# Attention values by halves of 64 queries: a 64-slot mask in place of a 128-slot one

## The chip, the cores and the metric

The kernel runs on one core of one Trainium2 chip. The metric is the time of one execution in microseconds of the device; the number to compare is the median of several runs. Engines are named as the profile names them: PE (matmul), PEld (its weight loads), DVE (vector), ACT (scalar), POOL (GpSimd) and SP (which issues most of the transfers). SBUF is the memory on the core, PSUM the accumulators that PE writes.

## The reference, cut to what matters

One decoder block on a sequence of 1024 tokens of width 1024: an adaptive norm, one wide projection, sliding-window attention with sinks in one branch and a gated recurrence in the other, both projected, merged and projected out. The change is in the attention: 16 query heads of 64, four key/value heads, each query sees itself and the 127 tokens before it.

```python
WINDOW = BLOCK = 128
qb = q.reshape(B, nb, BLOCK, N_KV_HEADS, G, hd)            # nb = 8 blocks of 128 queries, G = 4
kb = concat([kp[:, :-1], kp[:, 1:]], axis=2)               # the block's own keys and those before
s = einsum('bnqkgd,bnskd->bnkgqs', qb, kb) / sqrt(hd)      # 128 queries x 256 keys
diff = qi + BLOCK - kj
band = (diff >= 0) & (diff < WINDOW)                       # and kpos >= 0
s = where(mask, s, -1e30)
m = maximum(max(s, axis=-1), sink)
p = exp(s - m)
denom = sum(p, axis=-1) + exp(sink - m)
o = einsum('bnkgqs,bnskd->bnqkgd', p / denom, vb)
```

So each query has exactly 128 keys in its window (fewer in the first block), out of the 256 of its block and the one before.

## The kernel before, in words

Everything is in 32-bit floats; a product of two such operands is made of three PE products, since each operand is split into a high part and the rest (`split_a` on ACT casts, `split_d` on DVE subtracts). The order of instructions on PE, ACT, DVE, POOL and SP is the order of the source; tiles wait for each other by semaphores.

The kernel goes through the wide projection first (lines 688 to 776, 56 to 600 us), in "pairs" of weight chunks. Along with it, `v_prep(g)` takes the values of one key/value head group from the projection, and for each of eight blocks of 128 keys stores two tables in device memory: `vs` holds the values, and `dv` the difference between a block's values and those of the block before it. Both are `[128 keys, 8 blocks, 128]`: 64 columns of high parts and 64 of the rest. A row of a partition is 4 KB.

The attention has 32 units `u`: four groups `g`, in each eight blocks `n` of 128 queries. A unit does four heads. The loop over `u` (line 1626) is software-pipelined by hand; one turn holds, in the order in which the engines get them:

- `scores(u)`: eight PE products into one PSUM tile `s_ps` of 4 heads x 256 keys (for `n` = 0 only the last 128).
- `maxima_a(u)`: ACT copies the keys of the block itself out of PSUM into `p` (4 x 128 slots and one for the sink). `maxima_d(u)`: DVE puts over it, where the mask `mgt` says that the slot's own key is still to come, the key 128 earlier, which is in the same slot of the block before. So 256 keys become 128 slots, each with one key in the window. For `n` = 0 a POOL select writes -1e30 instead. Then DVE takes the maximum.
- `weights_a(u-1)`: ACT makes four exponentials with sums. `weights_d(u-1)`: DVE divides.
- a piece of another projection on PE (12 products of 512 columns), whose weights SP loads and ACT and DVE split.
- `values(u-3)`, `join_a`, `join_d`: the products with the values into PSUM tile `pv`, and the sum of its halves, ACT and DVE.
- `transposed(u-2)`, `split_a`, `split_d`: PE transposes the weights into PSUM tile `pt`, ACT and DVE split them into `phc` and `plc`.
- `masks(u-2)`: POOL selects the slots which hold a key of the block itself out of `phc` and `plc`, into `phm` and `plm`.

A slot's weight belongs to a key of the block before (value `vs` of that block) or of this one. So the values are one product of all weights with the former block's `vs`, and one of the masked weights with the difference `dv`, each for the high and the low part of the weights: four PE products of 512 columns (4 heads x 128 queries) with 128 slots in the contraction. For `n` = 0 all weights go with `dv` of block 0, two products. `load_v(m)` brings `vs` and `dv` for two units, issued from POOL's queue after `values`; `load_kq(m)` does so for keys and queries on SP's queue. The PSUM tiles `s_ps`, `pt` and `pv` exist once each.

The mask `mgt` is made by POOL early (lines 590 to 594), ahead of four loads of the rotary tables on POOL's queue.

Of the kernel before, what the change touches and what calls it, by code (L numbers as in the profile page):

```python
# [52 lines left out]
def tile_hybrid_block(ctx, tc, x, x_t, pk, rows, posr, posi, c_row, w_ss, w_gate, w_main, w_v,  # L53
# [72 lines left out]
    cs4_d = tc.dram_tile([24, 4, S], F32, name="cs4_d")  # L126
    k_d = tc.dram_tile([512, S], F32, name="k_d")
    v_d = tc.dram_tile([P, 8, NG, 64], F32, name="v_d")
    vs_d = [tc.dram_tile([P, 8, P], F32, name=f"vs_d{g}") for g in range(NG)]
    dv_d = [tc.dram_tile([P, 8, P], F32, name=f"dv_d{g}") for g in range(NG)]  # L130
    gate_d = tc.dram_tile([1, D], F32, name="gate_d")
    q_d = [tc.dram_tile([512, S], F32, name=f"q_d{g}") for g in range(NG)]
    ga_d = [tc.dram_tile([2, P, S], F32, name=f"ga_d{g}") for g in range(NG)]
# [440 lines left out]
    def operand_low(t):  # L574
# [3 lines left out]
        for lst, o in ((NT1, one), (NT3, two)) if t < 4 else ((NT4, one), (T2, two)):  # L578
# [7 lines left out]
    ctab = rpp.tile([P, S], F32, name="ctab")  # L586
    stab = rpp.tile([64, S], F32, name="stab")
    G.memset(ctab[64:128, :], 1.0)
    W["mgt"] = const.tile([P, P], U32, name="mgt")
    mf = rpp.tile([P, HALF], F32, tag="rh", name="mf", bufs=2)[:, :P]  # L590
    G.memset(mf, 1.0)
    G.affine_select(out=mf, in_=mf, pattern=[[1, P]], compare_op=ALU.is_gt, fill=0.0, base=0,
                    channel_multiplier=-1)
    G.tensor_copy(W["mgt"][:], mf)
# [595 lines left out]
    def v_prep(g):  # L1190
        t = {}
        vpp = W["vpp"]

        def f0():
            t["v"] = vpp.tile([P, 8, 64], F32, tag="v32", name="v32")
            dma(t["v"][:], v_d[:, :, g, :])

        def f1():
            t["d"] = vpp.tile([P, 8, 64], F32, tag="d32", name="d32")
            V.tensor_tensor(out=t["d"][:, 1:8, :], in0=t["v"][:, 1:8, :],  # L1200
                            in1=t["v"][:, 0:7, :], op=ALU.subtract)
            V.tensor_copy(t["d"][:, 0, :], t["v"][:, 0, :])

        def f2():
            for n_ in ("vs", "dv"):
                t[n_] = vpp.tile([P, 8, P], F32R, tag=n_, name=n_)
            A.copy(t["vs"][:, :, 0:64], t["v"][:])
            A.copy(t["dv"][:, :, 0:64], t["d"][:])

        def f3():  # L1210
            for n_, d_, dst in (("v", "vs", vs_d), ("d", "dv", dv_d)):
                V.tensor_tensor(out=t[d_][:, :, 64:128], in0=t[n_][:],
                                in1=f32(t[d_][:, :, 0:64]), op=ALU.subtract)
# [32 lines left out]
        dma(qs[:], q_d[g].rearrange("(a j) t -> a j t", j=4)[:, :, t0:t0 + 256])  # L1246
        U["kq", m] = ks, qs

    def load_v(m):
        g, n0 = m // 4, (m % 4) * 2  # L1250
        vs = at.tile([P, 2, P], F32R, tag="vs", name="vs", bufs=2)
        dv = at.tile([P, 2, P], F32R, tag="dv", name="dv", bufs=2)
        dma(dv[:], dv_d[g][:, n0:n0 + 2, :], G)
        lo = 0 if n0 else 1
        dma(vs[:, lo:, :], vs_d[g][:, n0 - 1 + lo:n0 + 1, :], G)
        U["v", m] = vs, dv

    def sink(u):
        px = at.tile([P, 4, P + 1], F32, tag="p", name="p", bufs=3)
# [19 lines left out]

    def maxima_a(u):  # L1280
        s_ps, px, sm = U["s", u]
        A.copy(px[:, :, 0:P], s_ps[:, :, P:])

    def maxima_d(u):
        s_ps, px, sm = U["s", u]
        p = px[:, :, 0:P]
        if u % 8:
            V.copy_predicated(p, W["mgt"][:].unsqueeze(1).to_broadcast([P, 4, P]),
                              s_ps[:, :, 0:P])
        else:  # L1290
            G.affine_select(out=p, in_=p, pattern=[[0, 4], [-1, P]], compare_op=ALU.is_ge,
                            fill=-1e30, base=0, channel_multiplier=1)
        V.tensor_reduce(out=sm[:, 0, :], in_=px[:], axis=AX.X, op=ALU.max, negate=True)

    def weights_a(u):
# [28 lines left out]
        U["m", u] = phc, plc  # L1324

    def masks(u):
        phc, plc = U["m", u]
        ms = []
        if u % 8:
            for s_, tag in ((phc, "phm"), (plc, "plm")):  # L1330
                d_ = at.tile([P, 4, P], F32R, tag=tag, name=tag)
                G.affine_select(out=d_[:], in_=f32(s_[:]), pattern=[[0, 4], [1, P]],
                                compare_op=ALU.is_ge, fill=0.0, base=0,
                                channel_multiplier=-1)
                ms.append(d_)
        U["m", u] = [phc, plc], ms

    def values(u):
        n = u % 8
        vs, dv = U["v", u // 2]  # L1340
        full, masked = U.pop(("m", u))
        prods = [((vs if n else dv)[:, n % 2, :], m) for m in full]
        prods += [(dv[:, n % 2, :], m) for m in masked]
        pv = psx.tile([P, 4 * P], F32, tag="v", name="pv")
        for i, (b, m) in enumerate(prods):
            W["pe"] = T.matmul(pv[:], b, m[:].rearrange("p j q -> p (j q)"),  # L1346
                               start=(i == 0), stop=(i == len(prods) - 1))
        U["pv", u] = [pv[:].rearrange("p (a e q) -> p a e q", a=2, e=2)]
        if n % 2 == 0 and u // 2 + 1 < 16:
            load_v(u // 2 + 1)  # L1350
# [275 lines left out]
    for u in range(32 + 3):  # L1626
# [458 lines left out]
```

## Time and profile before

| | us |
|---|---|
| median of 3 runs | 909.19 (907.67 to 910.17) |
| the profiled execution: time | 909.08 |
| its span on the core | 907.4 |
| PE busy | 889.1 |
| DVE busy | 725.8 |
| ACT busy | 554.9 |
| POOL busy | 124.7 |

The granted PE clock is 0.999 of full speed. The profile's page gives the busy time of each engine, the busy tenths of 40 slices of the span, the transfer queues, the chain of work that ended last (followed back from the end to what released each step), the costliest groups of instructions by line, and the transfers by size and time to landing. A group's row reads: line, engine, operation, output<-inputs, shapes, count | busy us, mean ns of one | idle time of the engine just before, and who ended it. Further views of the same execution give the chain in order of time, the instructions of one stretch, the waits, and the busy time by stretch.

### The profile page before, as it was taken

Reading aid. Unit: us, or ns where it says so; the run is one execution under the profiler, and the core shown is the slowest. Engines: PE = TensorE matmul, PEld = TensorE weight load, DVE = VectorE, ACT = ScalarE, POOL = GpSimd, SP = SyncE. Lnnn points to the kernel's source line nnn. Section 1 sums busy time; section 2 is a strip of 40 time slices with the busy share of each in tenths; the row PEclk is TensorE's granted clock in tenths of the full one; section 3 lists DMA queues with packets and bytes.
Section 4 is the critical chain, followed back from the end, with each engine's and each line's share of the span. In section 5 each row is a group of like instructions: output and inputs, shape, how many; then the busy total and the mean of one; then the engine's idle time right before and its main releaser. Section 6 shows DMA issues by size and latency. Waiting matters only on the chain.

```text
span 907.4 us, 12605 instructions
## 1 busy us (share of the span) xinstructions
PE 889.1 (98%) x4171; PEld 739.2 (81%) x4171; DVE 725.8 (80%) x1158; ACT 554.9 (61%) x1097; POOL 124.7 (14%) x204
## 2 busy tenths in 40 slices
PE   5999999999999999999999999999999999999997
PEld 3879888878888788878887888888888888888885
DVE  7988799698669974987698476899999846779875
ACT  6754675455556745774767685888888731114555
POOL 0120000000110000000100001354443421310002
PEclk9999999999999999999999999999999999999999
DMA  9951786862534360345345257996666258879314
GB/s 348 404 203 68 253 272 223 294 219 97 180 121 151 130 218 24 129 155 180 107 155 183 85 194 254 328 370 211 214 201 212 85 182 322 315 272 346 110 47 186
DMA packets 88882, 182.57 MB, mean 201 GB/s; under 512 B 14049, under 2 KB 30433, under 8 KB 88818
## 3 DMA queue, kind: packets, MB, share of 16 engines
q1 hardware_dynamic: 82192, 162.09, 51.8%
q0 software_dynamic: 6336, 19.37, 5.9%
q8 instruction: 33, 0.54, 0.3%
q10 hardware_dynamic: 290, 0.32, 0.1%
q14 instruction: 31, 0.25, 0.1%
HBM read 125.01 MB, written 57.12 MB: 201 GB/s over the span
## 4 chain that ended last, share of the span: by engine, by line
PE 86%; DVE 6%; DMA 3%; ACT 2%; issue 2%; SPq 0%; POOL 0%; DVEq 0%; ACTq 0%
PE bk L696 41%; PE rp L174 14%; PE bo L1857 7%; PE pmain L174 6%; PE pgate L992 5%; PE s_ps L1274 3%; PE pv L1346 3%; DMA r<-w_main 2%; PE pt L1312 2%; PE bk L174 1%; DVE wl L110 1%; PE bk L1520 1%; PE bk L1519 1%; PE bk L1518 1%; DMA wada<-w_ss 1%
## 5 line engine op out<-in xcount | busy, mean ns | idle before, releaser
L696 PE MATMUL bk<-nh,wl 128*128 128x512 f32 x368 | 143.9, 391 | 0.5 <-DVE wl L110 0.4
L696 PE MATMUL bk<-nh,wh 128*128 128x512 f32 x368 | 143.4, 390 | 0.0
L696 PE MATMUL bk<-nl,wh 128*128 128x512 f32 x368 | 143.2, 389 | 0.0
L696 PEld LDWEIGHTS bk<-nh,wl 128*128 128x128 f32 x368 | 69.1, 188 | 16.7 <-DVE wl L110 2.1
L696 PEld LDWEIGHTS bk<-nh,wh 128*128 128x128 f32 x368 | 69.1, 188 | 14.4 <-ACT rhi L626 0.2
L696 PEld LDWEIGHTS bk<-nl,wh 128*128 128x128 f32 x368 | 69.1, 188 | 14.4
L110 DVE TENSOR_TENSOR wl<-r,wh 128x512 fp32r<-128x512 f32 x112 | 80.1, 729 | 0.0
L60 POOL DMA_DIRECT2D wq_d<-wq x32 | 21.9, 685 | 407.2 <-DVE wq L1172 392.6
L104 ACT CAST wh<-r 128x512 fp32r<-128x512 f32 x112 | 68.0, 617 | 8.8 <-DMA r<-w_ap 5.1
L696 PE MATMUL bk<-hh,wh 128*128 128x512 f32 x184 | 71.6, 389 | 0.0
L696 PE MATMUL bk<-hh,wl 128*128 128x512 f32 x184 | 71.6, 389 | 0.0
L696 PE MATMUL bk<-hl,wh 128*128 128x512 f32 x184 | 71.6, 389 | 0.0
L110 DVE TENSOR_TENSOR wl<-ws,wh 128x512 fp32r<-128x512 f32 x80 | 54.8, 686 | 4.3 <-ACT wh L104 4.2
L104 ACT CAST wh<-ws 128x512 fp32r<-128x512 f32 x80 | 48.2, 614 | 3.3 <-PE bk L1520 2.7
L1298 ACT ACTIVATE p<-p,small 128x129 f32<-128x129 f32 x128 | 50.1, 401 | 0.0
L799 ACT ACTIVATE c<-bk 128x512 f32<-128x512 f32 x31 | 18.5, 595 | 44.0 <-PE bk L696 43.9
L696 PEld LDWEIGHTS bk<-hl,wh 128*128 128x128 f32 x184 | 34.5, 188 | 7.2
L696 PEld LDWEIGHTS bk<-hh,wl 128*128 128x128 f32 x184 | 34.5, 188 | 7.1
L696 PEld LDWEIGHTS bk<-hh,wh 128*128 128x128 f32 x184 | 34.5, 188 | 7.1
L1857 PE MATMUL bo<-wh,sum 128*128 128x512 f32 x128 | 39.6, 389 | 0.0
L1274 PE MATMUL s_ps<-ks,qs 128*128 128x256 f32 (+1 forms) x256 | 37.6, 289 | 0.0
L696 PE MATMUL bk<-hha,wl 128*128 128x512 f32 x92 | 36.1, 393 | 0.6 <-DVE wl L110 0.6
(409 smaller groups left out, 2290.1 us busy)
## 6 DMA issues: line engine op xcount, KB each, us to landing
r<-w_main SPq DMA_DIRECT2D x100, 256.0 KB, 4.3
wada<-w_ss SPq DMA_DIRECT2D x16, 512.5 KB, 9.3
qs<-q_d SPq DMA_DIRECT2D x16, 512.0 KB, 5.8
wq_d<-wq POOLq DMA_DIRECT2D x24, 256.0 KB, 2.8
wr<-wq_d SPq DMA_DIRECT2D x24, 256.0 KB, 5.0
ks<-k_d SPq DMA_DIRECT2D x24, 192.0 KB, 4.2
wq<-w_out POOLq DMA_DIRECT2D x16, 256.0 KB, 5.2
q_d<-rhi SPq DMA_DIRECT2D x16, 256.0 KB, 3.6
```

What stands on the lines that cost most here:

```text
L60: return eng.dma_start(dst, src)
L104: A.copy(dst[0][:], src)
L110: V.tensor_tensor(out=dst[1][:], in0=src, in1=f32(dst[0][:]), op=ALU.subtract)
L174: mm = T.matmul(ps[hf], ww, xx[kc][hf], start=(kc == 0 and ww is w_h and xx is xh), stop=(kc == KC - 1 and xx is xl))
L696: W["pe"] = T.matmul(ps, ww[:, c], b[kc][xx_], start=(first and kc == 0 and i == 0), stop=(kc == 3 and i == 2), skip_group_check=not first)
L799: A.activation(t["t"], s(), AF.Tanh, scale=0.5)
L992: W["pe"] = T.matmul(ps[:, SL[hf]], ww[:, c0:c0 + P], xx_[:, SL[hf]], start=(ic == 0 and i == 0), stop=(ic == 1 and i == 2))
L1274: W["pe"] = T.matmul(o, qs[:, j, qc], ks[:, b, k0 + (0 if n else P):k0 + 256], start=(b == 0), stop=(b == 1))
L1298: A.activation(px[:, j, :], px[:, j, :], AF.Exp, bias=sm[:, 0, j:j + 1], accum_out=sm[:, 1, j:j + 1])
L1312: W["pe"] = T.transpose(pt[:, j, :], px[:, j, 0:P], ident[:])
L1346: W["pe"] = T.matmul(pv[:], b, m[:].rearrange("p j q -> p (j q)"), start=(i == 0), stop=(i == len(prods) - 1))
L1857: T.matmul(bank[p][i] if dst is None else dst, a[:, ts_], b[:][:, sl], start=(new and kc == 0 and j == 0), stop=(kc == 3 and j == 2), skip ...
```

## The change

The 128 queries of a unit are taken as two halves of 64. A half has 128 slots again, but 64 of them hold keys that every query of the half sees; only the other 64 need a mask. For the first half of the queries the slots are keys 0 to 127 of the 256, for the second half keys 64 to 191; in both, slots 0 to 63 are overlaid with the 64 keys that follow, where those are in the window.

- Tables: `vs_d` and `dv_d` become `[18, 64, 128]` in device memory: 16 blocks of 64 keys, and two blocks of zeros ahead, which POOL's queue writes at the start from a `zero` tile. `v_prep` still makes 128-key blocks and stores them in pieces of one 512-byte row each.
- Loads: `load_v(u)` brings, for one unit, `vb` (per half of queries the 128 values in slot order; in the second half the two 64-key blocks lie swapped over the partitions) and `vd`, the differences, once on each half of the partitions. Four transfers per unit on SP's queue, three buffers, issued between `join_a` and `join_d`.
- `maxima_a`: two ACT copies, one for each half of the partitions (three for `n` = 0). `maxima_d`: two predicated DVE copies of 64 partitions x 4 heads x 64 keys, with the mask `mle`; for `n` = 0 a POOL memset and two POOL selects.
- `masks`: two POOL selects of 64 partitions, the high part into partitions 0 to 63 of one tile `cm`, the low part into 64 to 127. For `n` = 0 too.
- `values`: per half of queries one product of the high weights with `vb`, one of the low ones, and one of `cm` with `vd`, which does the high and the low part at once: six PE products of 256 columns (four for `n` = 0). Each reads 4 runs of 64 columns and writes 4 runs of 64.

```diff
-    vs_d = [tc.dram_tile([P, 8, P], F32, name=f"vs_d{g}") for g in range(NG)]
-    dv_d = [tc.dram_tile([P, 8, P], F32, name=f"dv_d{g}") for g in range(NG)]
+    vs_d = [tc.dram_tile([18, 64, P], F32, name=f"vs_d{g}") for g in range(NG)]
+    dv_d = [tc.dram_tile([18, 64, P], F32, name=f"dv_d{g}") for g in range(NG)]
...
-    W["mgt"] = const.tile([P, P], U32, name="mgt")
+    W["mle"] = const.tile([P, 64], U32, name="mle")
...
+    zero = rpp.tile([P, HALF], F32, tag="rl", name="zero", bufs=2)
+    G.memset(zero[:, :P], 0.0)
+    for g in range(NG):
+        dma(vs_d[g][0:2].rearrange("i r c -> (i r) c"), zero[:, :P], G)
...
-                dma(dst[g], t[d_][:])
+                dma(dst[g][2:].rearrange("(n b) r c -> (b r) n c", b=2), t[d_][:])
...
-    def load_v(m):
-        g, n0 = m // 4, (m % 4) * 2
-        vs = at.tile([P, 2, P], F32R, tag="vs", name="vs", bufs=2)
-        dv = at.tile([P, 2, P], F32R, tag="dv", name="dv", bufs=2)
-        dma(dv[:], dv_d[g][:, n0:n0 + 2, :], G)
-        lo = 0 if n0 else 1
-        dma(vs[:, lo:, :], vs_d[g][:, n0 - 1 + lo:n0 + 1, :], G)
+    def load_v(u):
+        g, i0 = u // 8, u % 8 * 2
+        vb = at.tile([P, 2, P], F32R, tag="vb", name="vb", bufs=3)
+        vd = at.tile([P, 2, P], F32R, tag="vd", name="vd", bufs=3)
+        for e in range(2):
+            half = slice(64 * e, 64 * e + 64)
+            dma(vb[half], vs_d[g][i0 + e:i0 + e + 2].rearrange("i r c -> r i c"))
+            dma(vd[half], dv_d[g][i0 + 2:i0 + 4].rearrange("i r c -> r i c"))
...
-        A.copy(px[:, :, 0:P], s_ps[:, :, P:])
+        for e in range(2):
+            r = slice(64 * e, 64 * e + 64)
+            if u % 8:
+                A.copy(px[r, :, 0:P], s_ps[r, :, 64 * e:64 * e + P])
+            else:
+                A.copy(px[r, :, 0:64], s_ps[r, :, P + 64 * e:192 + 64 * e])
+        if u % 8 == 0:
+            A.copy(px[64:P, :, 64:P], s_ps[64:P, :, P:192])
...
+        if u % 8 == 0:
+            G.memset(px[0:64, :, 64:P], -1e30)
+        for e in range(2):
+            r = slice(64 * e, 64 * e + 64)
+            p = px[r, :, 0:64]
+            if u % 8:
+                V.copy_predicated(p, W["mle"][r].unsqueeze(1).to_broadcast([64, 4, 64]),
+                                  s_ps[r, :, P + 64 * e:192 + 64 * e])
+            else:
+                G.affine_select(out=p, in_=p, pattern=[[0, 4], [-1, 64]], compare_op=ALU.is_ge,
+                                fill=-1e30, base=0, channel_multiplier=1)
...
-        if u % 8:
-            for s_, tag in ((phc, "phm"), (plc, "plm")):
+        cm = at.tile([P, 4, P], F32R, tag="cm", name="cm")
+        for i, s_ in enumerate(pieces):
+            G.affine_select(out=cm[64 * i:64 * i + 64].rearrange("p j (h q) -> p (j h) q", h=2),
+                            in_=f32(s_[0:64]).rearrange("p j (h q) -> p (j h) q", h=2),
+                            pattern=[[0, 8], [1, 64]], compare_op=ALU.is_ge, fill=0.0, base=0,
+                            channel_multiplier=-1)
...
+        prods = [(vb, m, h) for m in (phc, plc) for h in range(0 if u % 8 else 1, 2)]
+        prods += [(vd, cm, h) for h in range(2)]
+        for i, (b, m, h) in enumerate(prods):
+            c = slice(64 * h, 64 * h + 64)
+            W["pe"] = T.matmul(pv[:, :, c], b[:, h, :], m[:, :, c], start=(i == 0),
+                               stop=(i >= len(prods) - 2), skip_group_check=True)
...
             values(u - 3)
             join_a(u - 3)
+        if 1 <= u < 32:
+            load_v(u)
+        if u >= 3:
             join_d(u - 3)
```

More of the change, by code (lines that the diff above doesn't have):

```diff
@@ L588, in tile_hybrid_block @@
     G.memset(ctab[64:128, :], 1.0)
-    W["mgt"] = const.tile([P, P], U32, name="mgt")
+    W["mle"] = const.tile([P, 64], U32, name="mle")
     mf = rpp.tile([P, HALF], F32, tag="rh", name="mf", bufs=2)[:, :P]
[L591 to L594, printed above, removed]
+    G.memset(mf[:, 0:64], 1.0)
+    for e in range(2):
+        o = mf[64 * e:64 * e + 64, 0:64]
+        G.affine_select(out=o, in_=o, pattern=[[-1, 64]], compare_op=ALU.is_ge, fill=0.0, base=0,
+                        channel_multiplier=1)
+    G.tensor_copy(W["mle"][:], mf[:, 0:64])
+    zero = rpp.tile([P, HALF], F32, tag="rl", name="zero", bufs=2)
+    G.memset(zero[:, :P], 0.0)
+    for g in range(NG):
+        dma(vs_d[g][0:2].rearrange("i r c -> (i r) c"), zero[:, :P], G)
     for b in range(2):
@@ L1247, in load_kq @@
         U["kq", m] = ks, qs
-    def load_v(m):
-        g, n0 = m // 4, (m % 4) * 2
-        vs = at.tile([P, 2, P], F32R, tag="vs", name="vs", bufs=2)
-        dv = at.tile([P, 2, P], F32R, tag="dv", name="dv", bufs=2)
-        dma(dv[:], dv_d[g][:, n0:n0 + 2, :], G)
-        lo = 0 if n0 else 1
-        dma(vs[:, lo:, :], vs_d[g][:, n0 - 1 + lo:n0 + 1, :], G)
-        U["v", m] = vs, dv
+    def load_v(u):
[6 more added lines that the diff above has]
+            dma(vd[half], dv_d[g][i0 + 2:i0 + 4].rearrange("i r c -> r i c"))
+        U["v", u] = vb, vd
     def sink(u):
@@ L1281, in maxima_a @@
         s_ps, px, sm = U["s", u]
-        A.copy(px[:, :, 0:P], s_ps[:, :, P:])
+        for e in range(2):
[6 more added lines that the diff above has]
+            A.copy(px[64:P, :, 64:P], s_ps[64:P, :, P:192])
     def maxima_d(u):
         s_ps, px, sm = U["s", u]
-        p = px[:, :, 0:P]
-        if u % 8:
[L1288 to L1292, printed above, removed]
+        if u % 8 == 0:
+            G.memset(px[0:64, :, 64:P], -1e30)
+        for e in range(2):
+            r = slice(64 * e, 64 * e + 64)
[6 more added lines that the diff above has]
+                                fill=-1e30, base=0, channel_multiplier=1)
         V.tensor_reduce(out=sm[:, 0, :], in_=px[:], axis=AX.X, op=ALU.max, negate=True)
@@ L1326, in masks @@
     def masks(u):
-        phc, plc = U["m", u]
-        ms = []
-        if u % 8:
-            for s_, tag in ((phc, "phm"), (plc, "plm")):
[L1331 to L1336, printed above, removed]
-    def values(u):
[L1339 to L1350, printed above, removed]
+        pieces = U["m", u]
+        cm = at.tile([P, 4, P], F32R, tag="cm", name="cm")
[4 more added lines that the diff above has]
+                            channel_multiplier=-1)
+        U["m", u] = *pieces, cm
+    def values(u):
+        vb, vd = U.pop(("v", u))
+        phc, plc, cm = U.pop(("m", u))
+        pv = psx.tile([P, 4, P], F32, tag="v", name="pv")
+        prods = [(vb, m, h) for m in (phc, plc) for h in range(0 if u % 8 else 1, 2)]
[4 more added lines that the diff above has]
+                               stop=(i >= len(prods) - 2), skip_group_check=True)
+        U["pv", u] = [pv[:].rearrange("p (a e) q -> p a e q", a=2)]
     def join_a(u):
```

## The prediction

> **What bounds the kernel now.** I read the page's busy shares, then the chain that ended last, then that chain piece by piece in the attention stage, then the busy time by stretch, and last the instructions of single engines there.
>
> ```profile
> PE 889.1 (98%) x4171; PEld 739.2 (81%) x4171; DVE 725.8 (80%) x1158; ACT 554.9 (61%) x1097; POOL 124.7 (14%) x204
> ...
> PE 86%; DVE 6%; DMA 3%; ACT 2%; issue 2%; SPq 0%; POOL 0%; DVEq 0%; ACTq 0%
> ```
>
> TensorE is busy for 98% of the span and holds 86% of the chain, so a matmul removed is worth its slot in the queue, not its pipelined duration. The slots are in the pieces of the chain (start, length, what, count):
>
> ```profile
> 60.25 2.72 PE bk L174 x12
> ...
> 68.64 0.12 PE bk L1520
> ...
> 602.22 0.96 PE s_ps L1274 x8
> 603.18 2.75 PE rp L174 x12
> ```
>
> Twelve matmuls of 512 columns take 2.72 us: 0.227 us each. A 256-column one (L1520) takes 0.12 us with new weights each time, and eight score matmuls of 256 columns take 0.96 us, again 0.12 each.
>
> The change lies in the attention stage, about 560 to 732 us: one unit (128 queries, 4 heads) per turn, with a piece of the next projection between. By stretch (length, then busy time of PE, PEld, DVE, ACT, POOL, clock, DMA share):
>
> ```profile
> 560.00:600.00 40.00, 39.66 (x221) 33.97 (x220) 32.05 (x59) 33.02 (x103) 18.01 (x34) 1.00 1.04 348
> ...
> 602.22:692.20 89.98, 89.98 (x503) 77.40 (x502) 83.68 (x154) 73.83 (x239) 42.57 (x70) 1.00 0.69 222
> ...
> 712.00:732.00 20.00, 19.87 (x97) 16.23 (x96) 15.07 (x27) 12.05 (x34) 7.30 (x11) 1.00 0.16 53
> ```
>
> The middle stretch holds 18 units: 89.98/18 = 5.00 us each. PE has no idle there, but DVE is busy 83.68, which is 4.65 us per unit, and ACT 4.10. So PE binds with DVE just behind it. That is what this change has to be weighed on.
>
> **The change, part by part.**
>
> *Value products on PE.* A unit not first of its group had four matmuls of 512 columns and gets six of 256: 4 x 0.227 = 0.907 becomes 6 x 0.12 = 0.72, a gain of 0.187. A first unit has two of 512 and gets four of 256: 0.453 becomes 0.48, a loss of 0.027. With 28 and 4 units: 5.24 - 0.11 = 5.1 us less PE. Bounds: no gain below this, as six slots of 256 contiguous columns are the cheapest row; above, see the rival on strided output.
>
> *Mask copies on DVE.* One predicated copy of 128x512 becomes two of 64x256, one per half of the partitions.
>
> ```profile
> 627.04 0.69 DVE L1305 TENSOR_TENSOR p<-p,small 128x512 f32<-128x512 f32 x1
> 627.65 0.41 DVE L1366 TENSOR_TENSOR yq<-pv,ob 64x256 f32<-64x256 f32 x1
> 628.07 0.43 DVE L1367 TENSOR_TENSOR yq<-pv,ob 64x256 f32<-64x256 f32 x1
> 628.52 0.69 DVE L1323 TENSOR_TENSOR plc<-pt,phc 128x512 fp32r<-128x512 f32 x1
> 629.13 0.68 DVE L1482 TENSOR_TENSOR yq<-yq,r 128x512 f32<-128x512 f32 x1
> 629.73 0.75 DVE L1288 COPY_PREDICATED p<-mgt,s_ps 128x512 f32<-128x512 uint32 x1
> ```
>
> Halving the elements takes 0.69 only to about 0.42: 0.27 is saved and 0.15 is fixed. The group of the predicated copy has a mean of 739 ns (below), so a half costs about 0.74 - 0.27 = 0.47, the pair 0.93: +0.19 us per unit. Bounds: 0 (the pair at the old 0.74), and +0.74 (each half as long as the whole). I take +0.19, since the 64x256 rows show the fixed part on this very engine. The 0.69 us operations start 0.61 after one another, overlapping by 0.08, while the second 64x256 one starts 0.42 after a first that lasts 0.41; I let the pair not overlap. The Trainium skill has a model for that on the page "VectorE: DVE Perf Modes", section "Two Vector instructions with no wait between them": an instruction whose operands start in another group of 32 partitions than the last is held until the earlier ones have finished. The pair above (partitions 0 and 64) agrees; without that hold the pair would be 0.85 and the term +0.11.
>
> What DVE must do per unit today, in the same stretch, by groups (busy, mean ns, idle before):
>
> ```profile
> L1293 DVE TENSOR_REDUCE small<-p 128x4 f32<-128x516 f32 x19 | 13.1, 690 | 3.1 <-POOL p L1291 1.1 <-DVE p L1288 0.5
> ...
> L1288 DVE COPY_PREDICATED p<-mgt,s_ps 128x512 f32<-128x512 uint32 x16 | 11.8, 739 | 0.0
> L1282 ACT COPY p<-s_ps 128x512 f32<-128x512 f32 x18 | 10.6, 592 | 0.1
> ...
> L1366 DVE TENSOR_TENSOR yq<-pv,ob 64x256 f32<-64x256 f32 x18 | 7.4, 410 | 1.6 <-ACT ob L1356 1.4
> L1355 ACT COPY ob<-pv 64x256 f32<-64x256 f32 x19 | 7.0, 369 | 15.4 <-PE pv L1346 7.9 <-issue 6.1 <-ACT p L1298 1.5
> ...
> L1346 PE MATMUL pv<-phc,vs 128*128 128x512 f32 x16 | 6.2, 389 | 0.0
> ...
> L1346 PE MATMUL pv<-phc,dv 128*128 128x512 f32 x2 | 0.8, 389 | 0.0
> ```
>
> DVE's idle is 89.98 - 83.68 = 6.3 us, of which 1.4 + 1.1 + 0.5 = 3.0 are waits for others and 3.3 short gaps between dependent operations, which stay. So DVE needs (83.68 + 3.3)/18 = 4.83 us per unit. The last two rows count the values in the stretch: 16 ordinary units and 2 first ones. The sixteen add 0.19 each: 5.00 us. PE needs 5.00 - (16 x 0.187 - 2 x 0.027)/18 = 4.84. So in this stretch DVE takes over as the bound at the turn of today, and the PE gain shows as PE idle: term 0, with -2.9 (pair at the old price: all 16 x 0.187) and +3.0 (all three waits stay) as ends. The turns from 692 to 712 go the same way.
>
> *Copies on ACT.* One copy of 128x512 (592 ns) becomes two of 64x512. The 64x256 copies take 369, so by the free size 592 each: +0.59 per unit, bounds 0 and +0.59. ACT goes from 4.10 to 4.6 of 5.00 us; covered by the 15.4 us of idle ahead of L1355 (0.85 per unit). In a first unit three of 64x256 (1.1 us), one POOL memset and two half selects replace one copy and one select; DVE waits for that select already (1.1 us in two units): +0.3 over four units, between 0 and 2.
>
> *Masks on POOL.* Two selects per unit as before; the second now reads and writes half the partitions at the same free size, so I leave it its time. First units get two they had not, under POOL's idle. The end to keep is this one:
>
> ```profile
> 624.94 1.02 POOL L1332 TENSOR_SCALAR_AFFINE_SELECT plm<-plc 128x512 fp32r<-128x512 f32 x1 [1.06 <-DVE plc L1323]
> ...
> 626.31 0.39 PE L1346 MATMUL pv<-plm,dv 128*128 128x512 f32 x1
> ```
>
> The mask is done at 625.96, 0.35 us before its matmul, and in the new order it is wanted after 4 x 0.12 instead of 3 x 0.227, 0.2 sooner: 0.15 is left. Enough as long as DVE is not later than now.
>
> *Loads of values.* Two POOL loads per two units become four SP loads per unit, which wait for the values three units back; queued behind them on SP are the key and query loads and the projection's weights.
>
> ```profile
> 623.08 1.24 SPq L60 DMA_DIRECT2D ks<-k_d  x2
> 624.37 0.60 SPq L60 DMA_DIRECT2D qs<-q_d  x1
> ...
> vs_d<-vs SPq DMA_DIRECT2D x4, 512.0 KB, 4.9
> ...
> dv<-dv_d POOLq DMA_DIRECT2D x16, 128.0 KB, 5.3
> ...
> v<-v_d SPq DMA_DIRECT2D x4, 256.0 KB, 6.6
> ```
>
> At 0.6 us an issue that is 2.4 us of SP per 5.0, beside 1.84 per two units for keys and queries. Keys loaded at 623 serve scores two to three turns later, so 2.4 us is hidden: 0. Bytes double to 256 KB per unit, some 50 GB/s onto 222 at a share of 0.69: hidden here; the opening (share 1.04) has less room. The eight stores of values go from 4 KB rows to 512 B pieces, 1024 per store. The nearest such row is v<-v_d, 1024 pieces of 256 B: 6.6 us against 4.9 now.
>
> ```profile
> L60 SPq DMA_DIRECT2D vs_d<-vs x4: 381/400/447, 118.9 to 196.6; - x4
> ...
> 173.78 6.58 DMA r<-w_main
> ...
> 180.00:200.00 20.00, 19.83 (x85) 15.46 (x84) 19.41 (x36) 11.92 (x21) 0.00 (x0) 1.00 0.58 197
> ```
>
> They are issued between 119 and 197 us. A weight load is on the chain right behind the third pair of stores and PE idles 0.17 us after it, so a delay there reaches PE: between 0 and 2 x 1.7 = 3.4; I take +0.3, as the other three pairs have no such row.
>
> *Start.* Four stores of zeros go ahead of the rotary tables on POOL.
>
> ```profile
> 58.77 1.02 POOL L60 DMA_DIRECT2D ctab<-cs_d  x2
> ...
> L609 DVE TENSOR_TENSOR c<-c,ctab x5: 674/676/687, 91.4 to 188.4; 128x512 f32<-128x512 f32 x5
> ```
>
> At 0.51 each they delay the tables by 2 us, first read 30 us later: 0, bounds 0 and 0.
>
> **Sum.** The turn at 602.22 scores the tenth unit, and values come three turns after their scores: six units of values lie in the opening, 18 in the middle, eight behind. Opening, with DVE at 32.05 and ACT at 33.02 of 40: the PE gain arrives, 5 x 0.187 - 0.027 = -0.9. Middle and to 712: 0. Last four units, waiting on each other: between 0 and -0.75, taken as -0.4. First units +0.3, stores +0.3. Together -0.7 on the profiled execution's 909.08 us (span 907.4, 1.68 around it). The median of the runs is 909.19, 0.11 above: 908.5.
>
> **Rivals.** A: the above, 43%, 905.5 to 911.5.
>
> B: the pair of predicated copies costs no more than the one. Then DVE needs 4.83 and PE 4.84, and all 5.1 us of PE come through: 909.2 - 5.1 + 0.6 = 904.7. For it: PE is the bound today. Against: the 64x256 rows. 25%, 903.9 to 906.4.
>
> C, the other side: ACT. Every fourth turn it has a 1.02 us copy of rp, two casts and no slack:
>
> ```profile
> 697.70 1.02 ACT L1429 COPY rp<-rp 128x1024 f32<-128x1024 f32 x1
> ...
> 701.16 0.62 ACT L1487 CAST ah<-yq 128x512 fp32r<-128x512 f32 x1
> 701.79 0.37 ACT L1355 COPY ob<-pv 64x256 f32<-64x256 f32 x1
> ```
>
> No idle stands before that ob. With 0.59 more it comes 0.6 late, DVE's sum of pv and ob waits, and DVE, now full, cannot win it back: 0.6 per four turns over some 26 turns is +3.9, so 908.5 + 3.9 = 912.4. It decides once ob is later than DVE's own queue; below that it costs nothing. 19%, 910 to 914.
>
> D: the new matmuls read and write four runs of 64 columns instead of one run. If that made each as slow as one of 512 columns, a unit would cost 6 x 0.227 = 1.36 instead of 0.907: 28 x 0.455 + 4 x 0.455 = +14.6, so 923.8. The rows show only single runs (0.12), so nothing excludes it. The Trainium skill says on the page "Advanced Engine Details and Errata", section "PSUM Cachelines", that any non-contiguous pattern slows matmuls significantly, but also that two neighbouring elements should be contiguous, and here 64 are; no row here shows it. 6%.
>
> E: the 512 B pieces delay weight loads (stores) or the opening's loads by 2 to 4 us: 911 to 913. 7%.
>
> **Numbers.** About 0.3% (2.7 us) is what this kernel's runs can tell from no change: 906.5 to 911.9. Faster: B and 5 of A, 30%. Slower: D, 15 of C, 5 of E, 1 of A, 27%. The same: 43%. The range 904.0 to 913.3 leaves out D and the tails of B, C and E, some 16%.
>
> **What would show it.** Right: pv matmuls in six slots of 0.12; DVE over 97% busy in the middle stretch, two predicated copies near 0.47 each; PE idle there of about 0.15 per unit, ended by DVE or POOL cm; turns of 5.0. Wrong: predicated halves near 0.37 and turns of 4.84 (B); DVE idle before yq, ended by ACT ob, over 3 us (C); pv slots well over 0.12 (D); waits for r<-w_main near 180 us or for yh in the opening (E).

## The result, and the profile after

The changed kernel takes 922.22 us (median of 6 runs, 921.11 to 926.1) against 909.31 (907.67 to 912.55) for the kernel before on the same chip: a ratio of 1.0148, interval 1.0121 to 1.0175. It is slower by 1.5%, where no change was forecast and the range ended at 913.3. The profiled execution has a span of 920.3 us, before 907.4: 12.9 us to be found.

The page of the changed kernel, its busy shares and the chain that ended last:

```profile
PE 891.4 (97%) x4235; PEld 742.7 (81%) x4235; DVE 736.4 (80%) x1186; ACT 575.6 (63%) x1133; POOL 118.7 (13%) x194
...
PE 73%; DMA 8%; DVE 8%; ACT 6%; issue 3%; SPq 1%; POOL 1%; DVEq 0%; ACTq 0%; POOLq 0%
```

TensorE holds 73% of the chain where it held 86%. Transfers (8%, before 3%), DVE (8%, before 6%) and ACT (6%, before 2%) have taken the rest. To place the 12.9 us, I take the start of each unit's first score matmul in the two timelines. Unit 0 starts at 560.19 us before and 558.26 after; unit 3 at 571.62 and 570.52; unit 15 at 631.94 and 640.64; unit 31 at 711.67 and 724.38. Between them lie the stretches below (length, then busy time of PE, PEld, DVE, ACT and POOL, granted clock, DMA share, GB/s), the kernel before first:

```profile
571.62:631.94 60.32, 59.98 (x336) 51.31 (x334) 56.27 (x104) 50.79 (x163) 29.32 (x49) 1.00 0.95 318
631.94:711.67 79.73, 79.73 (x447) 68.66 (x446) 73.75 (x135) 65.86 (x213) 37.23 (x62) 1.00 0.60 190
```

and the changed one:

```profile
570.52:640.64 70.12, 63.58 (x357) 54.57 (x357) 61.25 (x116) 59.03 (x180) 25.84 (x42) 0.95 0.87 274
640.64:724.38 83.74, 80.13 (x480) 69.78 (x478) 78.68 (x147) 76.25 (x231) 33.16 (x54) 1.00 0.73 220
```

So there are two losses of different kinds. From unit 3 to unit 15 it is 70.12 - 60.32 = 9.8 us: PE is idle for 6.5 us, no compute engine is full, and the DMA share has gone *down* from 0.95 to 0.87. From unit 15 to unit 31 it is 83.74 - 79.73 = 4.0 us: here DVE has 4.9 us more to do. The rest is small: -1.9 before unit 0, +0.8 from unit 0 to 3, +0.2 behind unit 31; the sum is 12.9.

**The first loss: SP's queue.** Pieces of the chain of the changed kernel between 595 and 628 us (start, length, what):

```profile
595.07 8.65 DMA hl<-yl_d
603.71 0.02 issue
603.73 0.54 SPq L60
...
604.99 6.71 DMA hl<-yl_d
...
611.76 6.02 DMA r<-w_rp
617.78 0.02 issue
617.79 0.54 SPq L60
...
619.10 8.48 DMA yl<-yl_d
627.58 0.02 issue
627.59 0.57 SPq L60
```

A transfer lands, and at that moment SP issues something that has nothing to do with its data. What SP issued in between, from its timeline (start, length, transfer, how many):

```profile
595.07 0.84 SPq L60 DMA_DIRECT2D hl<-yl_d  x1
596.00 0.79 SPq L60 DMA_DIRECT2D vb<-vs_d  x1
596.89 0.59 SPq L60 DMA_DIRECT2D vd<-dv_d  x1
597.53 0.62 SPq L60 DMA_DIRECT2D vb<-vs_d  x1
598.21 0.60 SPq L60 DMA_DIRECT2D vd<-dv_d  x1
598.91 0.54 SPq L60 DMA_DIRECT2D r<-ga_d  x1
599.97 2.54 SPq L60 DMA_DIRECT2D ks<-k_d  x2
603.73 0.54 SPq L60 DMA_DIRECT2D qs<-q_d  x1
```

Count from hl at 595.07: four value loads, r, two of ks, and qs is the eighth. It starts 0.02 us after hl has landed. The same holds for the other three links: the eighth issue after hl at 604.99 is the second weight load at 611.76; the eighth after that is qs at 617.79; and the eighth after yl at 619.10 starts at 627.59. So this kernel has eight places for transfers on SP's queue, taken in order: an issue waits until the one eight before it has landed, whatever it is itself. The packed trace shows what the places are. SP's transfers signal eight semaphores (counters that an engine can wait for) in turn. For 591 of the 609 times that one is used again, the issue itself or an instruction of SP just ahead of it waits for that same semaphore. So the eight are the program's own; how many transfers the chip would let run, no run tells.

Four of each eight places went to the values. The load of qs for units 12 and 13, which was issued at 604.50 before, goes out at 617.79 and lands 4.8 us later, at 622.6. The scores of unit 12 need it:

```profile
622.82 2.04 PE L1281 MATMUL s_ps<-ks,qs 128*128 128x256 f32 x8 [2.98 <-DVE yq L1381]
```

PE stands for 2.98 us ahead of them. The view names DVE's yq, which the scores don't read; in the packed trace, PE's wait for the semaphore that the landing of qs raises ends at 622.60.

That pause costs twice. Busy time by stretch of the changed kernel, with the granted clock as the third column from the right:

```profile
619.70:622.80 3.10, 0.13 (x2) 0.01 (x1) 2.89 (x8) 2.27 (x8) 0.97 (x2) 0.84 0.84 285
622.80:625.00 2.20, 2.18 (x9) 2.19 (x10) 2.20 (x3) 0.10 (x1) 0.98 (x1) 0.50 1.04 355
625.00:629.00 4.00, 4.00 (x11) 3.10 (x10) 2.49 (x6) 3.21 (x11) 0.00 (x0) 0.54 0.37 84
```

After 3.1 us with PE nearly idle, the clock is 0.50 to 0.54 for 6.2 us: one unit's eight score matmuls and twelve of the projection take 622.82 to 629.27, 6.45 us, instead of 0.96 + 2.75: 2.7 us more. The Trainium skill says on the page "TensorE: Matmul & The Clock Gate", section "Part 1: The HAM clock gate (the "warmup" mystery)", that the clock halves after an idle window of about 3.4 us. Here less was enough: PE stood for 2.98 us, and the mean of 0.84 in the first row means some 1.0 of its 3.1 us at 0.50, so the clock fell about 2 us after PE's last matmul.

**The second loss: DVE.** Groups of the changed kernel from unit 15 to 31 (busy, mean ns, idle before):

```profile
L1292 ACT COPY p<-s_ps 64x512 f32<-64x512 f32 x28 | 16.3, 582 | 1.6 <-PE s_ps L1281 1.5
L1323 DVE TENSOR_TENSOR p<-p,small 128x512 f32<-128x512 f32 x16 | 13.0, 811 | 0.5
L1306 DVE COPY_PREDICATED p<-mle,s_ps 64x256 f32<-64x256 uint32 x28 | 12.7, 455 | 0.2
L110 DVE TENSOR_TENSOR wl<-r,wh 128x512 fp32r<-128x512 f32 x8 | 9.1, 1135 | 0.0
```

The predicated pair is 0.91 us a unit where one copy took 0.74: over 28 rows 12.7 against 10.3, +2.4 us, as forecast. But two groups that the change doesn't touch are dearer too: the weights' product (L1323, before 692 ns) by 16 x 0.119 = 1.9 us, and wl (L110) by 8 x 0.123 = 1.0. Its row before:

```profile
L110 DVE TENSOR_TENSOR wl<-r,wh 128x512 fp32r<-128x512 f32 x8 | 8.1, 1012 | 0.0
```

The timeline of the changed kernel shows why:

```profile
667.09 0.65 POOL L1348 TENSOR_SCALAR_AFFINE_SELECT cm<-phc 64x512 fp32r<-64x512 f32 x1 [0.74 <-ACT phc L1335]
667.14 1.14 DVE L1323 TENSOR_TENSOR p<-p,small 128x512 f32<-128x512 f32 x1
...
670.00 0.98 POOL L1348 TENSOR_SCALAR_AFFINE_SELECT cm<-plc 64x512 fp32r<-64x512 f32 x1 [2.26 <-DVE plc L1341]
670.39 1.14 DVE L110 TENSOR_TENSOR wl<-r,wh 128x512 fp32r<-128x512 f32 x1
```

A product with both inputs in SBUF that starts while POOL's select runs takes 0.98 to 1.14 us instead of 0.69. In this stretch that happens to five of the weights' products (before: none) and to all eight of wl (before: six). The Trainium skill says on "SBUF — State Buffer", section "SBUF: two separate sides", that such an operation and one of GpSimd share a pair of ports, and the later one is held until the first has finished. The first select ends at 667.74; 0.69 after that is 668.43, and the product ends at 668.28, so the row agrees to 0.15 us.

DVE's idle time in the stretch is 5.1 us, of which only 2.1 are waits for other engines. The loss is uneven: six of the sixteen turns take 4.84 to 4.86 us, less than the 5.04 of before, and the others up to 6.08.

### The profile page after: what moved, and what is told of

It is laid out like the page before. It is cut to its first block, busy times and chain, and to the rows that moved or that the text cites. A ratio compares the mean times of both kernels' runs of the same rounds, so it can differ in the third digit from the quotient of the medians.

```text
span 920.3 us, 13174 instructions
## 1 busy us (share of the span) xinstructions
PE 891.4 (97%) x4235; PEld 742.7 (81%) x4235; DVE 736.4 (80%) x1186; ACT 575.6 (63%) x1133; POOL 118.7 (13%) x194
## 4 chain that ended last, share of the span: by engine, by line
PE 73%; DMA 8%; DVE 8%; ACT 6%; issue 3%; SPq 1%; POOL 1%; DVEq 0%; ACTq 0%; POOLq 0%
PE bk L702 38%; PE rp L174 10%; PE bo L1874 7%; PE pmain L174 6%; PE pgate L998 5%; DMA r<-w_main 2%; DMA hl<-yl_d 2%; PE s_ps L1281 2%; SPq L60 1%; PE pv L1362 1%; DVE wl L110 1%; PE bk L174 1%; DMA yl<-yl_d 1%; DMA wada<-w_ss 1%; PE bk L1534 1%
## 5 line engine op out<-in xcount | busy, mean ns | idle before, releaser
L110 DVE TENSOR_TENSOR wl<-r,wh 128x512 fp32r<-128x512 f32 x112 | 81.2, 738 | 0.0
L110 DVE TENSOR_TENSOR wl<-ws,wh 128x512 fp32r<-128x512 f32 x80 | 54.6, 683 | 1.2 <-ACT wh L104 1.2
L1281 PEld LDWEIGHTS s_ps<-ks,qs 128*128 128x128 f32 x256 | 33.2, 194 | 8.8 <-ACT ob L1370 3.5
```

What stands on the lines that cost most here:

```text
L110: V.tensor_tensor(out=dst[1][:], in0=src, in1=f32(dst[0][:]), op=ALU.subtract)
L1281: W["pe"] = T.matmul(o, qs[:, j, qc], ks[:, b, k0 + (0 if n else P):k0 + 256], start=(b == 0), stop=(b == 1))
```

## The experiments

**Two theories.** T1: the first loss is the number of issues on SP's queue; rival T1b: it is the bytes, or their 512 B pieces. T2: the second loss is DVE's, by the pair (T2a) or by pair and collisions together (T2b); rival: ACT's pair of copies. Each run is read by its stretches, unit 3 to 15 and unit 15 to 31, measured as above in one profiled execution. Five kernels have the four loads a unit on SP (changed, e3, e10, e11, e13); they take 70.12 to 74.78 us from unit 3 to 15, so a difference of that size there tells nothing.

| kernel | us, median | ratio to before (interval) | unit 0 starts | unit 3 to 15 | unit 15 to 31 |
|---|---|---|---|---|---|
| before | 909.31 | | 560.19 | 60.32 | 79.73 |
| changed | 922.22 | 1.0148 (1.0121, 1.0175) | 558.26 | 70.12 | 83.74 |
| e1, loads on POOL | 922.83 | 1.0158 (1.0143, 1.0173) | 560.19 | 67.59 | 84.12 |
| e3, old mask copies | 920.4 | 1.013 (1.0108, 1.0153) | 560.49 | 71.62 | 78.30 |
| e4, both | 929.29 | 1.0233 (1.0216, 1.025) | 560.87 | 68.51 | 85.37 |
| e5, before, loads on SP | 923.42 | 1.0162 (1.0147, 1.0177) | 559.33 | 73.78 | 79.74 |
| e6, two loads a unit | 926.55 | 1.0186 (1.0168, 1.0205) | 564.58 | 65.85 | 84.06 |
| e7, one load a unit | 921.59 | 1.0142 (1.0111, 1.0173) | 573.81 | 60.50 | 78.24 |
| e8, the same on POOL | 922.66 | 1.0153 (1.0114, 1.0191) | 573.78 | 60.71 | 78.18 |
| e9, before, tiny loads | 920.98 | 1.0156 (1.0121, 1.0191) | 558.40 | 72.88 | 79.70 |
| e10, one predicated copy | 920.89 | 1.0126 (1.0105, 1.0147) | 559.03 | 74.78 | 79.54 |
| e11, one ACT copy | 925.57 | 1.0175 (1.0153, 1.0196) | 559.39 | 72.09 | 83.30 |
| e12, table built in DRAM | 914.68 | 1.0065 (1.0044, 1.0086) | 563.93 | 61.97 | 78.22 |
| e13, no selects | 919.9 | 1.0108 (1.0089, 1.0127) | 559.93 | 71.64 | 79.39 |

**e5: the kernel before, its value loads on SP.**

```
-        dma(dv[:], dv_d[g][:, n0:n0 + 2, :], G)
-        dma(vs[:, lo:, :], vs_d[g][:, n0 - 1 + lo:n0 + 1, :], G)
+        for i in range(2):
+            for e in range(2):
+                half = slice(64 * e, 64 * e + 64)
+                dma(dv[half, i, :], dv_d[g][half, n0 + i, :])
+                if i >= lo:
+                    dma(vs[half, i, :], vs_d[g][half, n0 - 1 + i, :])
```

> The kernel before, its matmuls, masks and copies untouched; only its value loads are moved from POOL's queue (two per two units) to SP's and cut into eight per two units of 32 KB each, the same bytes in all and whole pieces of 512 B. T1 (number of SP issues and transfer places): slower by 6 to 10 us, to 915-919, with the loss between units 3 and 15. T1b (bytes and not issues): within 1 us of before, 908-910.

Measured 923.42, and nearly all of the loss in the stretch that T1 names: 73.78 us from unit 3 to 15, +13.5, and 79.74 behind it, as before. PE waits 9.6 us there for the value loads themselves, which now stand in SP's queue. No matmul, mask or copy of the change is in this kernel. Its chain between 600 and 622 us:

```profile
601.56 9.33 DMA hl<-yl_d
...
610.90 0.45 SPq L60
```

The issue at 610.90 is again the eighth after hl. T1 holds in place and kind; the size is larger than the 6 to 10 I gave.

**e9: the kernel before, with eight loads of 2 KB for every two units.**

```
+        for i in range(8):
+            t = at.tile([64, 8], F32, tag=f"tiny{i}", name="tiny")
+            dma(t[:], v_d[0:64, i, 0, 0:8])
```

> The kernel before, and for every two units eight loads more on SP's queue, of 64 x 8 elements (2 KB) into tiles that nothing reads; its value loads stay on POOL. It tells the time of an issue on SP from the places that long transfers hold: if SP's time is what is short (eight issues of 0.45 to 0.6 us per two units), it loses as much as the run whose value loads were moved to SP in eight, 10 to 15 us; if the places are short and a small transfer frees its place early, it loses 0 to 4.

Measured 920.98, +12.6 us from unit 3 to 15. By my own expectation that would make SP's time the cause, but SP's timeline says otherwise:

```profile
588.47 0.65 SPq L60 DMA_DIRECT2D qs<-q_d  x1
589.17 9.25 SPq L60 DMA_DIRECT2D tiny<-v_d  x8
598.46 0.58 SPq L60 DMA_DIRECT2D hh<-yh_d  x1
```

```profile
588.47 9.49 DMA qs<-q_d
```

Eight tiny issues take 9.25 us, not eight times 0.45, and the last of them can go when qs has landed at 597.96. SP waits; its time isn't short. What I had wrong is that a small transfer frees its place early: places are taken in turn, so each tiny load waits for the long one eight before it, and moves almost no bytes while it does. What comes late is again qs, and PE stands for 5.33 us ahead of the scores that need it:

```profile
625.92 2.05 PE L1277 MATMUL s_ps<-ks,qs 128*128 128x256 f32 x8 [5.33 <-DMA qs<-q_d]
```

T1b falls for the bytes: from 570 to 640 us this kernel moves 18.20 MB, the one before 21.20 MB, and it still loses 12 us. Pieces of 512 B are no need of the loss either: the value loads keep the pieces they had before, and the tiny loads' own are of 32 B.

**e6 and e7: fewer and larger loads on SP.** e6 loads a unit's values in two transfers, from tables in which all 128 partitions lie at one stride:

```
-        for e in range(2):
-            half = slice(64 * e, 64 * e + 64)
-            dma(vb[half], vs_d[g][i0 + e:i0 + e + 2].rearrange("i r c -> r i c"))
-            dma(vd[half], dv_d[g][i0 + 2:i0 + 4].rearrange("i r c -> r i c"))
+        w = vs_d[g][i0:i0 + 2].rearrange("i r c -> (i r) c")
+        dma(vb[:], bass.AP(tensor=w.tensor, offset=w.offset, ap=[[P, P], [64 * P, 2], [1, P]]))
+        dma(vd[:], dv_d[g][i0:i0 + 2].rearrange("i e r c -> (e r) i c"))
```

> The changed kernel with two value loads of 128 KB a unit on SP's queue instead of four of 64 KB: the same bytes in the same 512 B pieces into the same tiles (one table lies twice in DRAM, so that both halves of the partitions come with one load; that makes twelve more stores, before 200 us). Theory T1 (eight transfer places on SP's queue, and each load takes one): half the extra places, so the stretch from unit 3 to unit 15 takes 62 to 66 us instead of 70.1, the total is 914 to 919; the steady 83.7 from unit 15 to 31 stay. Rival (bytes or pieces are what delays): 920 to 924.

e7 takes e3 (below) and one transfer a unit, from a table with all four slots side by side:

```
-        vb = at.tile([P, 2, P], F32R, tag="vb", name="vb", bufs=3)
-        vd = at.tile([P, 2, P], F32R, tag="vd", name="vd", bufs=3)
...
+        vv = at.tile([P, 4, P], F32R, tag="vv", name="vv4", bufs=3)
+        dma(vv[:], vt_d[u // 8][:, u % 8])
```

> The old copies out of PSUM and four selects a unit (as in the earlier run without the pair of copies), and one load of 256 KB a unit on SP's queue, from a table that holds all four slots side by side (2 KB pieces; stores of the table on POOL's queue, 16 half stores a group, before 200 us). T1: one extra place a unit is nearly nothing, the stretch from unit 3 to 15 takes 60 to 62 us, unit 15 to 31 78.3, the total 906 to 909. Rival (bytes): 918 to 921, as with four loads.

With the same bytes a unit, four, two and one load give 70.12, 65.85 and 60.50 us from unit 3 to 15 (four loads without the predicated pair, e3: 71.62). That is T1's order (65.85 lies below all five kernels with four loads), with the pieces of 512 B unchanged from four loads to two (e7 has pieces of 2 KB), and one load a unit is nearly free. What is left in e6 is hardly SP's: from unit 3 to 15 PE waits there 0.6 us for a load of ks, but 1.7 us for the mask cm and 2.3 us for ACT and DVE. So the second loss reaches into the opening, where the two overlap: e3, without the pair, loses no less.

Both totals missed, for a reason of my own making: the stores of the larger tables. Unit 0 starts 4.4 us late in e6 and 13.6 late in e7 (which stores from POOL's queue, eight half stores a group and not the sixteen that I wrote). Two stretches of e8, whose stores are those of e7:

```profile
120.00:140.00 20.00, 16.90 (x73) 13.36 (x72) 16.93 (x29) 10.57 (x19) 3.19 (x5) 1.00 0.95 291
180.00:200.00 20.00, 12.02 (x43) 9.38 (x42) 9.77 (x18) 6.26 (x11) 0.00 (x0) 0.74 0.62 214
```

PE is idle for 3.1 and 8.0 us there, where the kernel before had 0 and 0.17.

**e1, e4 and e8: POOL's queue instead.** e1 is the changed kernel with its four loads a unit issued by POOL, e4 the same on e3's kernel, e8 the one load of e7 on POOL:

```
-            dma(vb[half], vs_d[g][i0 + e:i0 + e + 2].rearrange("i r c -> r i c"))
-            dma(vd[half], dv_d[g][i0 + 2:i0 + 4].rearrange("i r c -> r i c"))
+            dma(vb[half], vs_d[g][i0 + e:i0 + e + 2].rearrange("i r c -> r i c"), G)
+            dma(vd[half], dv_d[g][i0 + 2:i0 + 4].rearrange("i r c -> r i c"), G)
```

> The changed kernel with one edit: the four value loads of a unit are issued from POOL's queue instead of SP's. Theory T1 (the loss between unit 3 and unit 15, 9.8 us, comes from SP's queue: four more issues per unit fill its eight transfer places and put off the weight and key loads behind them): that loss goes, the stretch takes 60 to 62 us again, the time falls by 8 to 10 us, to 912-914. Rival T1b (the loss comes from the bytes, twice as many in 512 B pieces, not from the queue they are issued on): nothing moves, 921-923. T2 (DVE is over-full in the steady turns because of the split mask copies and the selects beside its sums) predicts that the 4.0 us of unit 15 to 31 stay in this run either way.

> Old mask copies and four selects as in the run before, and the value loads on POOL's queue. T1 and T2 together: both losses go and the gain of TensorE's queue (0.187 us a unit) comes through in part: 904 to 907. If only T1 holds: 912-914; if only T2 holds: 917-918; if the two causes cover each other (the sum of the single gains is larger or smaller than this one), the difference to e1 and e3 says so.

> As the run before, the one load a unit on POOL's queue, which then has as many issues as in the kernel before (two per two units of 0.6 us). T1 and T2: both losses gone, unit 15 to 31 78.3 to 79, the total 905.5 to 908, so faster than before by 0.1 to 0.4%. If POOL's in-order wait for the values of three units back holds up the four selects: turns of 5.0 or more in the steady part, 909 to 912.

e1 and e4 missed: 922.83 and 929.29. In e1 unit 15 to 31 keeps its loss (84.12), as expected, but unit 3 to 15 takes 67.59 us and not 60 to 62: PE waits 4.5 us there for the mask cm. Leaving SP wasn't enough, as four issues are too many for POOL as well. e4 from unit 15 to 31, and the shares of its chain by line between 600 and 640 us:

```profile
642.47:727.84 85.37, 82.72 (x480) 70.86 (x478) 73.71 (x134) 65.97 (x213) 77.17 (x146) 1.00 0.66 204
```

```profile
by line: POOL cm L1338 31.8%; POOL vd L60 19.6%; POOL vb L60 15.3%; issue 11.7%; PE rp L174 6.9%; POOL p L1268 5.7%; PE pv L1351 2.9%; PE s_ps L1280 2.4%; DVE small L1299 1.7%; POOL p L1297 1.6%; PE pt L1318 1.1%; DVE small L1310 0.2%; POOL
```

POOL is busy for 77.17 of 85.37 us: four issues of 0.60 us and four selects a unit, and the selects, which the value products wait for, stand behind the issues. With one issue a unit (e8) the stretch takes 78.18 and the opening 60.71, as with e7. The steady part of the expectation for e8 holds; its total fails by the table's stores.

**e3, e10, e11 and e13: DVE.** e3 takes the old copies out of PSUM back, leaves the slots unswapped and selects four 64x256 blocks:

```
-                V.copy_predicated(p, W["mle"][r].unsqueeze(1).to_broadcast([64, 4, 64]),
-                                  s_ps[r, :, P + 64 * e:192 + 64 * e])
+            V.copy_predicated(p, W["mgt"][:].unsqueeze(1).to_broadcast([P, 4, P]),
+                              s_ps[:, :, 0:P])
...
-            dma(vb[half], vs_d[g][i0 + e:i0 + e + 2].rearrange("i r c -> r i c"))
+            dma(vb[half], vs_d[g][i0:i0 + 4].rearrange("(n b) r c -> b r n c", b=2)[0] if e == 0
+                else vs_d[g][i0 + 1].unsqueeze(1).to_broadcast([64, 2, P]))
```

> The changed kernel with the old copies out of PSUM (one ACT copy and one predicated DVE copy of 128 partitions x 512), the slots not swapped (values loaded in a matching order by the same four SP loads), and the masks as four POOL selects of 64 x 256. The six half matmuls and the SP loads stay. T2 (steady turns bound by DVE and its pair of mask copies): unit 15 to 31 takes 79 to 81 us instead of 83.7, the total falls by 4 to 5 us, to 917-918, with the opening's loss untouched. Rival (the steady loss is SP's too, DVE's pair only lies beside it): unit 15 to 31 stays at 83 or more, the total at 921-923. A further rival (the pair on ACT is what counts) gives the same as T2 here and is told apart by waits: DVE sums waiting for ACT's ob over 3 us.

e10 changes the predicated copy alone, e11 the ACT copy alone, and e13 makes the diagonal mask once:

```
e10  +            V.copy_predicated(px[:, :, 0:P], W["mgt"][:].unsqueeze(1).to_broadcast([P, 4, P]),
     +                              s_ps[:, :, 0:P])
e11  +            A.copy(px[:, :, 0:P], s_ps[:, :, P:])
e13  +        for i, s_ in enumerate(pieces if u == 0 else ()):
```

> The changed kernel with one predicated copy of 128 x 512 on DVE instead of two of 64 x 256; it takes the wrong slots for the second half of the queries, so that part of the weights is left out of the computation; the two copies on ACT, the masks and the four SP loads stay. T2a (the pair on DVE is the steady loss, 0.17 us a unit, and the slower sums beside POOL's selects are only its companions): unit 15 to 31 takes 79 to 80 us. T2b (half of the loss is the pair, half are DVE sums that run longer while POOL's selects run): 81 to 82. Rival (ACT's pair is what counts): 83 or more. The opening's loss stays in any case.

> The changed kernel with one copy of 128 x 512 on ACT instead of two of 64 x 512 (the second half's slots are then not the swapped ones, so part of the scores is left out of the computation); the predicated pair on DVE stays. T2a and T2b: ACT is off the path, unit 15 to 31 stays at 83 to 84 us. Rival (rival C of the prediction, ACT's 0.59 us a unit): 79 to 81.

> The changed kernel whose diagonal mask is made once, for unit 0, and read again by all others: POOL's two selects a unit, and the matmul's wait for them, are left out of the computation. T2b: DVE's sums go back to 0.69 us, the pair stays, unit 15 to 31 takes 81 to 82 us. T2a: it stays near 83, as the pair is still there. Should it fall below 80, the pair costs nothing by itself and the selects are the whole steady loss.

From unit 15 to 31, in the order e3, e10, e11, e13:

```profile
643.58:721.88 78.30, 78.14 (x479) 69.37 (x478) 72.23 (x135) 66.00 (x213) 41.08 (x82) 1.00 0.76 231
```

```profile
645.79:725.33 79.54, 79.02 (x479) 69.55 (x478) 73.93 (x135) 76.26 (x231) 33.98 (x54) 1.00 0.78 231
```

```profile
642.95:726.25 83.30, 80.06 (x480) 69.64 (x478) 78.02 (x146) 67.56 (x217) 33.59 (x54) 1.00 0.74 222
```

```profile
643.88:723.27 79.39, 78.13 (x479) 69.24 (x478) 74.14 (x147) 75.85 (x231) 8.11 (x22) 1.00 0.76 231
```

e11 shortens ACT by 8.7 us and the stretch by 0.4: ACT's pair costs next to nothing. e10, with the selects kept, wins 4.2 us; e13, with the pair kept, wins 4.35. By itself e10 says that the pair is the whole loss, and e13 that the selects are. So the loss isn't a sum of two prices. DVE is busy for 78.7 us of 83.74, and ten of the sixteen turns are longer than the 4.85 us that PE needs; either way takes DVE to about 74, where PE (98 to 99% busy in both) sets the pace again. In e10 the pair's 2.4 us go, and the weights' product is back at 692 ns: without the pair it no longer starts into the first select. In e13 it is back at 692 ns as well, and wl falls to 737:

```profile
L1323 DVE TENSOR_TENSOR p<-p,small 128x512 f32<-128x512 f32 x16 | 11.1, 692 | 0.5
...
L110 DVE TENSOR_TENSOR wl<-r,wh 128x512 fp32r<-128x512 f32 x8 | 5.9, 737 | 0.0
```

e13 takes away more than the change had added: wl was at 1012 ns in the kernel before, so 2.2 us of what DVE saves were there already. And with the selects goes PE's wait for the mask, 1.3 us in the changed kernel, so e13 alone doesn't tell that wait from the longer sums. In e10 the selects are kept, and that wait falls to 0.2 us: so the wait follows from what the pair makes late. That both runs win the same because DVE was too full is argued from these rows; no run changes DVE's work alone without moving its sums against the selects.

e3 ends at 78.30, a little under the 79 to 81 expected; its total of 920.4 is not the 917 to 918 expected, as the opening takes 71.62. It is 1.4 us ahead of the kernel before: that is what the half matmuls bring to a stretch that PE binds. Nine of its sixteen turns take 4.83 to 4.86 us instead of 5.04, the 0.19 of the forecast; the others, up to 5.12 us, keep the sum below the 14 x 0.187 - 2 x 0.027 = 2.6 us of the slots.

**e12: both losses out, the table built in DRAM.** e8 with the stores of the kernel before; 32 copies on POOL's queue build the table later:

```
+                dma(dst[g], t[d_][:])
...
+            dma(vt_d[g][r, lo:, s if v else s + 2],
+                (vs_d if v else dv_d)[g][64 * half:64 * half + 64, 0:8 - lo], G)
```

> The run with one load a unit on POOL's queue, but the values stored as in the kernel before, and the table of four slots built by 32 copies from DRAM to DRAM on POOL's queue between about 300 and 470 us, where the DMA share is 0.36. If the 13.6 us that the run with the table's stores lost before unit 0 came from those stores at 120 to 240 us, unit 0 starts at 560 to 561 again, and with turns of 4.89 the total is 906.5 to 908.5, ahead of the kernel before by 0.1 to 0.2%. If the copies delay the weights that the projections load at that time: 910 to 916.

914.68: faster than the changed kernel, slower than before by 0.65% (0.44 to 0.86). The total is in the second range of the expectation. The steady 78.22 holds. Unit 0 starts 3.7 us late, as the copies began at 271 us already, not at 300, and 21 of the 32 went out within 22 us:

```profile
240.00:300.00 60.00, 56.88 (x243) 46.16 (x242) 41.56 (x57) 35.35 (x50) 18.45 (x27) 0.97 0.57 200
```

PE is idle for 3.1 us of these 60, waiting for DVE and ACT to split weights. From unit 3 to 15 1.65 us are lost too: PE waits 1.7 us for qs, and the chain has an hl load of 11.84 us. Why, no run tells, as e7 and e8 load the same bytes and lose 0.2 and 0.4. No version that was run beats the kernel before.

## Why the prediction was wrong

- **The step that failed first** is "Keys loaded at 623 serve scores two to three turns later, so 2.4 us is hidden: 0". The 0.6 us an issue was right (medians of 0.59 and 0.60 measured). But I asked only whether SP's time fits into a turn and whether its data is early enough. What bound was how many transfers the program lets be under way: keys and queries that were issued two to three turns early before came just as their scores wanted them, or later. That can be seen before the change: among SP's waits between 565 and 645 us in the kernel before (us in total, times, longest) stand landings of transfers that nothing on SP reads, under the large one for its own buffer:

```profile
SPq L60 <- PE s_ps L1274: 35.0, 8, 6.7
...
SPq L60 <- DMA ks<-k_d: 1.4, 4, 0.7
...
SPq L60 <- DMA hl<-yl_d: 1.1, 1, 1.1
```

Those 35 us were the room (the row of the scores in the changed kernel reads 1.0), and eight issues more per two units used it up. Term 0, measured 9.8 us, of which some 2.7 are the clock after the pause and a part is the second loss. Rival E came nearest (the opening's loads delayed, 2 to 4 us, 7%), but gave the 512 B pieces as its reason; e9 shows the loss with the value loads untouched.
- **The second** is the middle stretch, "term 0" with an upper end of +3.0: measured +4.0 over sixteen units. That DVE takes over as the bound was right, and the pair's price too (0.47 each forecast, 455 ns measured; the pair takes 0.92 us in the timeline, twice that, so the two don't overlap: the hold that the Trainium skill states on "VectorE: DVE Perf Modes", section "Two Vector instructions with no wait between them", agrees). The term left out that the pair pushes DVE's sums into POOL's selects; a row of it stood in the groups that I read, from 602 to 692 us before: wl at 1023 ns, while its like al takes 681. I took that as its price. e10 and e13 show that pair and selects make the loss together. So two of the signs that I had listed did not come: DVE is busy for 94% of the stretch and not over 97%, and the turns are not 5.0 but 4.84 to 6.08 us.
- **Right:** six value products in slots of 0.12 us (chain of the changed kernel below), so rival D (923.8 us by slow strided matmuls) falls. Of the two rules that the Trainium skill gives on "Advanced Engine Details and Errata", section "PSUM Cachelines", the one for two contiguous neighbours agrees: runs of 64 cost nothing. ACT's pair at 582 ns is hidden (e11), so rival C falls. Rival B falls with the pair's price.

```profile
639.73 0.72 PE pv L1362 x6
```

- **Small terms:** the stores were taken at +0.3: PE is busy for 19.95 of 20 us from 180 to 200 us, against 19.83 before, so 0. The mask's lead of 0.15 us was too thin: between unit 15 and 31 the value products wait 1.3 us in all for POOL's select (their weight loads 2.8), a part of the 4.0. The 50 GB/s onto 222 counted the old bytes twice, since half of the 256 KB a unit was in the 222 already; the stretch from unit 15 to 31 goes from 190 to 220 GB/s. That unit 0 starts 1.9 us earlier need not be the change's gain: e9, whose edit adds nothing but the tiny loads of the attention, has 558.40.

## What to carry to other kernels

Count issues, not only bytes and issue time: where transfers take 5 to 9 us and the program lets eight of a queue run, each further load, however small, pushes the loads behind it later, so load more per transfer before moving a load to another queue. When a bound engine gets 0.17 us more per turn, ask which operations of a neighbour it will now overlap: an engine with 6 to 8% to spare can lose as much to that as to the added work. And lay tables out so that one transfer fetches them, but price the stores that build them: here they cost more than the loads had.

## What was not expected of the hardware

- A load of 2 KB holds a place in SP's queue as one of 512 KB does: eight of them kept SP for 9.25 us. The releaser is each time the landing of an earlier transfer; the eight are the program's own semaphores, and how many the chip would let run, no run tells.
- A pause of PE of 2.98 us brought the granted clock to 0.50 to 0.54 for the next 6.2 us; it fell some 2 us into the pause.
- A DVE product of two SBUF inputs takes 0.69 us alone and up to 1.14 when it starts into a POOL select; one that starts ahead of the select keeps its 0.69.
